# Moving the weight splits of a decoder trunk from GpSimd to VectorE, with a fifth pair of split slots

## The chip, the core and the metric

The kernel runs on one core of a Trainium2 chip. The metric is the device time of one execution in microseconds (us). The engines are TensorE (PE in the profile; PEld is its weight load), VectorE (DVE), ScalarE (ACT), GpSimd (POOL) and the queue SP, which issues the transfers from HBM.

## What is computed

A two-layer decoder trunk on 256 tokens of width 1024, all in float32. Cut to what matters here:

```python
for layer in range(2):
    main = short_conv_mixer(...) if layer == 0 else moba_attention(...)   # 12 x 64 wide
    mem_out = memory_cross_attention(q_mem, mem_k, mem_v)                 # 4 heads
    mix = concat([main, mem_out]) @ w_o[layer]
    x = layer_norm(alpha * x + mix, ln1_g[layer], ln1_b[layer])
    ffn = swiglu(x, w_gu_dense, w_down_dense) if layer == 0 else moe_swiglu(x, ...)  # top 2 of 8
    x = layer_norm(alpha * x + ffn, ln2_g[layer], ln2_b[layer])
    if layer == 0:
        shared = shared_key_value(x, w_kv_shared, cos, sin)
```

## The kernel before

**Products.** All products before the experts are made from numbers that are split in two parts: a value is `hi + lo`, each of which TensorE multiplies in one fast pass, and a product is hi·hi + lo·hi + hi·lo. Activations are split as they are made (`split`, L222). Weights are split piece by piece: a piece is 128 x 2048 numbers (1 MB). The experts, from the last norm on, take their weights whole and are not split.

**The stream of weights.** The class `Stream` (L67) holds the list of all pieces in the order of their use. A piece is loaded by SP into a raw slot (`load`), cast to `hi` by ScalarE (`high`, L129), and its `lo = raw - hi` is made by a subtraction (`low`, L139), which frees the raw slot and issues the next load. `hi` and `lo` together are a pair of split slots; there are 3 raw slots and 4 pairs (3 in `ring`, a fourth, `split4`, in `act`), and in the dense stage 2 more raw slots (`raw1`, L631). `done` frees a pair after the last product with the piece and calls `pump`, which makes as many `high` and `low` as there are free pairs, with the newest `low` left for the next call (`lag`). `held` stops `pump`; `lows` makes up all outstanding `low`; `step` makes one `high` and its `low`; `get` hands out the next piece. A pair that comes free after the last split becomes two raw slots for the experts, unless it was retired. All engines work through their instructions in the order of the program.

**Which engine subtracts.** `low` runs on VectorE, or on GpSimd while the counter `spare` is positive; `spare` is set to 2 ahead of the norms of the first layer (L643, L722) and to 8 in the attention stage (L816) and ahead of the last norm (L850). In the first step of the experts, `row_parts(0)` (L905) makes the `lo` of 128 token rows on GpSimd, `row_parts(1)` on VectorE.

**The stages around the change.** Tokens come in two blocks of 128 rows, block 0 and block 1.

- Output projection of layer 0 and its norm (L629 to L653): four pieces; the last two for block 0 first, then `layer_norm(x1[:, 0])` on VectorE while TensorE does block 1, then `layer_norm(x1[:, 1])`. TensorE goes on with `mem_keys`, in whose middle it turns block 0 (`trans_split`), and with `mem_values`, at whose end it turns block 1.
- Dense SwiGLU (L707 to L716): 11 groups of two up pieces and one down piece.
- The last three down pieces and the second norm (L717 to L732): the same pattern. After `layer_norm(x2[:, 0])` block 0 is turned, the keys' product of block 0 begins, and in its third piece block 1 is turned (task of L790).
- Keys, queries (L786 to L807), value rows with the first attention units (L815 to L819), output projection of layer 1 with the other units (L821 to L853). A unit is a pair of heads: `scores` (maximum on VectorE, exponentials on ScalarE, scaling on VectorE), `transp`, `values`. The units and `trans_split` share four PSUM banks (`bank`, L61).
- The last norm, the router and eight experts (from L848). Here raw slots are also the pools `raw2`, `raw3` and `raw5`.

Of the kernel before, what the change touches and what calls it, by code (L numbers as in the profile page):

```python
# [45 lines left out]
def trunk_kernel(ctx: ExitStack, tc: tile.TileContext, x, mem, positions, w_in_a, conv_a, w_q_b,  # L46
                 w_kv_shared, w_mem_kv, w_o, ln1_g, ln1_b, ln2_g, ln2_b, w_gu_dense, w_down_dense,
                 w_router, w_gu_moe, w_down_moe, out):
    nc = tc.nc
    pool = lambda n, **k: tc.tile_pool(name=n, bufs=1, **k)  # L50
# [16 lines left out]
    class Stream:  # L67
# [4 lines left out]
        def __init__(self):  # L72
            self.specs, self.parts, self.raw = [], {}, {}
            self.pools, self.split_pools, self.home, self.turned = [], [], {}, {}
            self.n_dma = self.n_hi = self.n_lo = self.n_got = self.n_done = 0
            self.held = False
            self.spare, self.lag = 0, 1
            self.n_split = 0

        def add(self, *specs):  # L80
# [52 lines left out]
        def low(self):  # L133
            raw, n, p = self.raw.pop(self.n_lo)
            q = self.home[self.n_lo]
            lo = q[0].tile([P, PC], F32R, name="lo", tag="lo" + q[1], bufs=q[4])
            hi = self.parts[self.n_lo][0]
            v = lo[:, :n].rearrange("p (a b) -> p a b", a=hi.shape[1])
            (nc.gpsimd if self.spare > 0 else nc.vector).tensor_sub(  # L139
                v, raw[:, :n].rearrange("p (a b) -> p a b", a=hi.shape[1]), hi)  # L140
            self.spare -= 1
            self.parts[self.n_lo].append(v)
            self.n_lo += 1
            p[3] -= 1
            self.load()
# [91 lines left out]
    def trans_split(src, hi, lo, tb, halves=(0, 1)):  # L237
        for h in halves:
            pt = bank()
            for i in range(4):  # L240
                nc.tensor.transpose(pt[:, i * P:(i + 1) * P], src[:, (4 * h + i) * P:(4 * h + i + 1) * P],
                                    identf)
            ptv = pt.rearrange("p (a b) -> p a b", a=4)
            split(hi[:, 4 * h:4 * h + 4, tb * P:(tb + 1) * P], lo[:, 4 * h:4 * h + 4, tb * P:(tb + 1) * P], ptv)

    def last(gen, tasks=(), every=1):

        tasks, v = list(tasks), None
        for i, v in enumerate(gen):
            if i % every == every - 1 and tasks:  # L250
                t = tasks.pop(0)
                if t:
                    t()
        for t in tasks:
            if t:
                t()
        return v

    def prod_ws(n, nb, ah, al):

        v = [b.rearrange("p (i t) -> p i t", i=2) for b in banks(nb // 2)]
        kt = 0
        for _ in range(n):
            w_hi, w_lo = st.get()[0]
            for k in range(w_hi.shape[1]):
                for i in range(nb):
                    w_h, w_l = w_hi[:, k, i * P:(i + 1) * P], w_lo[:, k, i * P:(i + 1) * P]
                    mm(v[i // 2][:, i % 2], w_h, ah[:, kt], start=(kt == 0 and i % 2 == 0))
                    mm(v[i // 2][:, i % 2], w_h, al[:, kt], start=False)
                    mm(v[i // 2][:, i % 2], w_l, ah[:, kt], start=False)  # L270
                kt += 1
                if k + 1 < w_hi.shape[1]:
                    yield v
            st.done()
            yield v
# [75 lines left out]
    def layer_norm(dst, old, add, gb, mid=None):  # L351
        mv = small.tile([P, 1, 2], F32, name="ln_mv", tag="ln_mv", bufs=2)
        stats = ln_sums(dst, old, add)
        if mid:
            mid()
        nc.vector.bn_aggr(mv[:, 0], stats)
        z = ln_scale(mv, 1)
        for h in range(2):
            ln_apply(dst, slice(h * 512, (h + 1) * 512), mv[:, 0, 0:1], z, gb)
# [263 lines left out]
    def wo_prod(l, dst, pc, i, tb, done, **kw):  # L623
        k0 = W_O_ORDER[l][i]
        sl = slice(tb * P, (tb + 1) * P)
        last(prod_ts(dst, pc, lambda k: mh[:, k0 + k, sl], lambda k: ml[:, k0 + k, sl], first=(i == 0), done=done,
                     **kw))

    x1 = res.tile([P, TB, D], F32, name="xt", tag="xt", bufs=2)  # L629
    more = ExitStack()  # L630
    raw1 = st.slots(more.enter_context(pool("more")), "raw1", 2)  # L631
    st.load()
    dst = [banks(), banks()]
    pcs = []
    for i in range(2):
# [4 lines left out]
    for i in (2, 3):  # L640
        wo_prod(0, dst[0], pcs[i], i, 0, False, outer=(i == 3))
    st.lows()
    st.spare = 2  # L643
    layer_norm(x1[:, 0], xt[:, 0], dst[0], gb)
    for i in (2, 3):
        wo_prod(0, dst[1], pcs[i], i, 1, True, outer=(i == 3))
    st.lows()
    with st.hold():
        layer_norm(x1[:, 1], xt[:, 1], dst[1], gb,
                   lambda: mem_keys([None] * 5 + [lambda: trans_split(x1[:, 0], xh, xl, 0)]))  # L650
        gb = ln_vectors(act, ln2_g[0], ln2_b[0])
        mem_values(tasks2=[None] * 7 + [lambda: trans_split(x1[:, 1], xh, xl, 1)])
# [18 lines left out]
    def down(g, pc, tb, done, **kw):  # L671
        hh, hl = hT[g]
        sl = slice(tb * P, (tb + 1) * P)
        last(prod_ts(dn[tb], pc, lambda k: hh[:, k, sl], lambda k: hl[:, k, sl], first=(g == 0), done=done,
                     **kw))
# [31 lines left out]
    for g in range(NG):  # L707
        up(g)
        if g == 2:
            rope_tables()  # L710
        if g == NG - 2:
            st.retire(raw1)
        if 0 < g <= NG - TAIL:
            pc = st.get()[0]
            for tb in range(TB):
                down(g - 1, pc, tb, tb == 1)  # L716
# [2 lines left out]
    for i in range(TAIL):  # L719
        down(NG - TAIL + i, pcs[i], 0, False, outer=(i == TAIL - 1))  # L720
    st.lows()
    st.spare = 2  # L722
    layer_norm(x2[:, 0], x1[:, 0], dn[0], gb)
    for i in range(TAIL):
        down(NG - TAIL + i, pcs[i], 1, i < TAIL - 1, outer=(i == TAIL - 1))
    st.lows()
    layer_norm(x2[:, 1], x1[:, 1], dn[1], gb, lambda: trans_split(x2[:, 0], xh, xl, 0))
    st.done()
    st_ffn.close()
    st.drop(raw1)  # L730
    more.close()
    gb = ln_vectors(act, ln1_g[1], ln1_b[1])  # L732

# [22 lines left out]
    def rope(pt, tb):  # L756
        t = att.tile([P, 12, HD], F32, name="roped", tag="roped", bufs=2)
        a = att.tile([P, 12, 2, 8], F32, name="rot")
        tf = t.rearrange("p h d -> p (h d)")
        nc.scalar.copy(tf[:, :512], pt[0])  # L760
        nc.scalar.copy(tf[:, 512:], pt[1][:, :MIX - 512])
        for s in range(2):
            nc.vector.tensor_tensor(a[:, :, s], t[:, :, 8 * (1 - s):8 * (1 - s) + 8],
                                    sn[:, tb, s][:, None, :].to_broadcast([P, 12, 8]), op=OP.mult)
        nc.vector.tensor_tensor(t[:, :, 0:16], t[:, :, 0:16],
                                cs[:, tb].rearrange("p a b -> p (a b)")[:, None, :].to_broadcast([P, 12, 16]),
                                op=OP.mult)
        nc.vector.tensor_tensor(t[:, :, 0:16], t[:, :, 0:16], a.rearrange("p h a b -> p h (a b)"), op=OP.add)
        return tf
# [13 lines left out]
    def turn_task(store, tb, i0, n, keys):  # L783
        return lambda: turn_heads(store[tb], tb, i0, n, keys)
# [3 lines left out]
    for tb in range(TB):  # L788
        pt = banks()
        last(token_prod(pt, pcs, tb, late=(tb == 0)), [] if tb else [None] * 9 + [lambda: trans_split(x2[:, 1], xh, xl, 1)])  # L790
        kt[tb] = rope(pt, tb)
    v = last(prod_ws(1, 2, xh, xl), [None, turn_task(kt, 0, 0, 4, True), None, turn_task(kt, 0, 4, 2, True)])
    nc.scalar.copy(qm, v[0])
    units = mem_units(att)
# [18 lines left out]
        nc.vector.tensor_copy(vb[:, tb, 512:], pt[1][:, :MIX - 512])  # L813

    u = units[2:]  # L815
    st.spare = 8  # L816
    value_rows(0, [None, None, None, None, None, turn_task(qt, 1, 0, 4, False), turn_task(qt, 1, 4, 2, False), None,
                   u[0].scores, None, None, None, u[1].scores])
    value_rows(1, [None, u[0].transp, None, None, u[2].scores, None, None, u[1].transp])  # L819
# [27 lines left out]
    st.load()  # L847
    x3 = res.tile([P, TB, D], F32, name="xt", tag="xt", bufs=2)  # L848
    wo_prod(1, dst[0], pcs[3], 3, 0, False, outer=True)
    st.spare = 8  # L850
    layer_norm(x3[:, 0], x2[:, 0], dst[0], gb)
    wo_prod(1, dst[1], pcs[2], 2, 1, True)
    wo_prod(1, dst[1], pcs[3], 3, 1, True, outer=True)  # L853
# [48 lines left out]

    def row_parts(tb):
        nc.scalar.copy(xth[:, tb], x3[:, tb])
        (nc.vector if tb else nc.gpsimd).tensor_sub(xtl[:, tb], x3[:, tb], xth[:, tb])  # L905

    def select():
        other, own = lg[:, :, None, :].to_broadcast(T4), lg[:, :, :, None].to_broadcast(T4)
# [86 lines left out]
    def experts(part):  # L995
# [159 lines left out]
        def first_step(gathers):  # L1155
            pt = banks(2)
            first_columns(pt[0], 0, 0, KT)
            logits(0)
            turn_rows(1)
            first_hidden(0, pt[0])  # L1160
            logits(1)
            select()
            row_parts(1)
            row_parts(0)
            first_columns(pt[1], 1, 0, 6)
            number()
            count()
            first_columns(pt[1], 1, 6, KT)
            for _ in range(2):
                st.passed()  # L1170
            gathers[0]()
            choose()
            for t in gathers[1:1 + KT]:
                t()
            load_orders()
            first_hidden(1, pt[1])
            load_count(0)
# [121 lines left out]
```

## Time and profile before

| | us |
|---|---|
| median of 3 runs | 1166.44 (1165.89 to 1167.29) |
| the profiled execution | 1166.54 |
| its span, first to last instruction | 1164.7 |
| TensorE, share of the span with a matmul running | 93% |
| VectorE, ScalarE, GpSimd | 33%, 22%, 6% |
| span until the first expert's products | about 477 |

How to read it: a row of the timeline gives the start in us from the span's start, the duration, the engine, the line of the kernel, the operation, the tile written and the tile read, and in brackets how long the engine sat idle ahead of it and what ended that idle time. PEclk is the granted clock of TensorE as a share of its full 2.4 GHz; its other level in this trace is 1.2 GHz (0.5).

### The profile page before, as it was taken

To read this page: it belongs to the slowest core of one execution; us is meant where nothing else is said; L and a number is where in the kernel's file an instruction comes from. 1 tells how busy PE (TensorE), PEld (TensorE's weight loads), DVE (VectorE), ACT (ScalarE), POOL (GpSimd) and SP (SyncE) were. 2 spreads that over 40 slices of the span, in tenths; PEclk is the share of its full clock that TensorE was granted. 3 is DMA by queue.
4 is the path that set the end of the run, shared out by engine and by line. 5 is a ranking of instruction groups with operands and counts; after the bars stand their busy time and mean duration, and the time that the engine had idled before them with its cause. 6 is when DMAs were issued, how large, how long until landed. Compare 5 with 4: busy or idle time off the path is not lost. (4 is left out here: it accounts for less than half of the span.)

```text
span 1164.7 us, 17138 instructions
## 1 busy us (share of the span) xinstructions
PE 1082.7 (93%) x6958; PEld 643.8 (55%) x6958; DVE 386.6 (33%) x607; ACT 256.0 (22%) x379; POOL 69.8 (6%) x55
## 2 busy tenths in 40 slices
PE   8999899999989889998988999899999999999992
PEld 7988899999877656444522443344333343343331
DVE  5767656444776566310100100101110101110105
ACT  4553443443335342110100100100100100100100
POOL 1002100000120330100000000000000000000001
PEclk9999999999989989999999999999999999999996
DMA  9646655555243239889999999989999999989992
GB/s 330 215 178 221 210 186 181 175 187 195 95 153 131 86 103 382 351 329 408 406 406 408 407 406 409 400 328 398 391 404 409 406 406 408 406 345 401 407 404 81
DMA packets 127589, 353.78 MB, mean 304 GB/s; under 512 B 6375, under 2 KB 41968, under 8 KB 127488
## 3 DMA queue, kind: packets, MB, share of 16 engines
q1 hardware_dynamic: 127392, 352.35, 79.6%
q8 instruction: 69, 1.13, 0.4%
q14 instruction: 32, 0.26, 0.1%
q0 software_dynamic: 96, 0.04, 0.0%
HBM read 351.32 MB, written 1.05 MB: 303 GB/s over the span
## 5 line engine op out<-in xcount | busy, mean ns | idle before, releaser
L65 PE MATMUL pa<-raw,xg 128*64 128x512 f32 (+4 forms) x2304 | 388.8, 560 | 9.8 <-DMA raw<-in_w_gu_moe_dram 9.3
L65 PEld LDWEIGHTS pa<-raw,xg 128*64 128x64 f32 (+1 forms) x2304 | 140.3, 129 | 245.8 <-issue 212.4
L65 PE MATMUL pb<-raw,hT 128*64 128x512 f32 x704 | 158.8, 601 | 6.9 <-ACTq L1194 2.9
L129 ACT CAST hi<-raw 128x2048 fp32r<-128x2048 f32 (+2 forms) x68 | 124.7, 1836 | 139.2 <-PE pa L65 96.8
L65 PE MATMUL pa<-xh,hi 128*128 128x256 f32 x528 | 150.0, 284 | 0.2 <-ACT xh L223 0.2
L65 PE MATMUL pa<-xl,hi 128*128 128x256 f32 x528 | 148.8, 282 | 0.3 <-DVE xl L224 0.3
L65 PE MATMUL pa<-xh,lo 128*128 128x256 f32 x528 | 148.6, 281 | 0.0
L1060 DVE TENSOR_TENSOR h<-h,pa 128x512 f32<-128x512 f32 (+2 forms) x24 | 15.3, 637 | 400.3 <-PE pa L65 388.8
L139 DVE TENSOR_TENSOR lo<-raw,hi 128x2048 fp32r<-128x2048 f32 (+2 forms) x60 | 130.5, 2181 | 48.8 <-ACT hi L129 48.8
L65 PEld LDWEIGHTS pb<-raw,hT 128*64 128x64 f32 x704 | 49.9, 138 | 102.2 <-issue 89.9
L1059 ACT ACTIVATE h<-pa 128x512 f32<-128x512 f32 (+2 forms) x24 | 13.4, 557 | 408.8 <-PE pa L65 408.8
L65 PEld LDWEIGHTS pa<-xh,hi 128*128 128x128 f32 x528 | 100.2, 190 | 1.6 <-issue 0.8
L65 PEld LDWEIGHTS pa<-xl,hi 128*128 128x128 f32 x528 | 100.2, 190 | 0.9 <-DVE xl L224 0.5
L65 PEld LDWEIGHTS pa<-xh,lo 128*128 128x128 f32 x528 | 100.1, 190 | 0.0
L139 POOL TENSOR_TENSOR lo<-raw,hi 128x2048 fp32r<-128x2048 f32 x8 | 37.7, 4726 | 370.0 <-ACT hi L129 263.1
L1207 POOL MEMSET yh<- 32x1024 f32 x8 | 7.6, 944 | 626.9 <-PE pb L65 617.5
L65 PE MATMUL pb<-raw,hTx 128*32 128x256 f32 x704 | 40.3, 380 | 3.9 <-DVE hTx L1096 3.9
L224 DVE TENSOR_TENSOR yl<-pb,yh 64x512 fp32r<-64x512 f32 (+1 forms) x32 | 17.7, 555 | 69.0 <-ACT yh L223 69.0
L65 PE MATMUL pa<-hi,xh 128*128 128x512 f32 (+1 forms) x96 | 36.1, 376 | 0.0
L1078 DVE TENSOR_TENSOR hx<-hx,pa 64x512 f32<-64x512 f32 (+1 forms) x12 | 7.8, 646 | 82.5 <-ACT hx L1077 65.3
L65 PEld LDWEIGHTS pb<-raw,hTx 128*32 128x32 f32 x704 | 22.5, 110 | 21.4 <-DVE hTx L1096 4.4
L65 PE MATMUL pa<-lo,xh 128*128 128x512 f32 (+1 forms) x96 | 33.5, 349 | 0.0
(238 smaller groups left out, 1054.7 us busy)
## 6 DMA issues: line engine op xcount, KB each, us to landing
raw<-in_w_gu_moe_dram SPq DMA_DIRECT2D x128, 1024.0 KB, 17.9
raw<-in_w_down_moe_dram SPq DMA_DIRECT2D x88, 1024.0 KB, 16.6
raw<-in_w_gu_moe_dram SPq DMA_DIRECT2D x56, 768.0 KB, 15.7
raw<-in_w_gu_dense_dram SPq DMA_DIRECT2D x44, 512.0 KB, 4.9
raw<-in_w_down_dense_dram SPq DMA_DIRECT2D x11, 1024.0 KB, 5.1
raw<-in_w_in_a_dram SPq DMA_DIRECT2D x8, 1024.0 KB, 9.9
raw<-in_w_o_dram SPq DMA_DIRECT2D x8, 1024.0 KB, 4.8
raw<-in_w_kv_shared_dram SPq DMA_DIRECT2D x6, 1024.0 KB, 5.1
```

What stands on the lines that cost most here:

```text
L65: nc.tensor.matmul(o, l, r, start=start, stop=stop, skip_group_check=True)
L129: nc.scalar.copy(hi[:, :n], raw[:, :n])
L139: (nc.gpsimd if self.spare > 0 else nc.vector).tensor_sub(v, raw[:, :n].rearrange("p (a b) -> p a b", a=hi.shape[1]), hi)
L224: nc.vector.tensor_sub(lo, src, hi)
L1059: nc.scalar.activation(h[:, :w], pg[:, :w], AF.Silu)
L1060: nc.vector.tensor_tensor(h[:, :w], h[:, :w], pu[:, :w], op=OP.mult)
L1078: nc.vector.tensor_tensor(h[64:, :w], h[64:, :w], px[64:, :w], op=OP.mult)
L1207: nc.gpsimd.memset(t[HALF:CAP].bitcast(F32), 0.0)
```

## The change

It makes all `low` run on VectorE (the counter `spare` is gone) and `row_parts(0)` too, which also moves to an earlier place. The two extra raw slots of the dense stage give way to a fifth pair of split slots of the same size (`split5`), which is the first to be filled. Between the two norms of a sub-layer of layer 0 no split is made: `held` is set ahead of the first norm, for the first sub-layer until block 1 has been turned, for the second until the keys' product of block 0 and its `rope`; there, one `step` stands between the sums and the rest of the second norm.

```diff
@@ low @@
-            (nc.gpsimd if self.spare > 0 else nc.vector).tensor_sub(
+            nc.vector.tensor_sub(
                 v, raw[:, :n].rearrange("p (a b) -> p a b", a=hi.shape[1]), hi)
-            self.spare -= 1
@@ first sub-layer @@
-    raw1 = st.slots(more.enter_context(pool("more")), "raw1", 2)
-    st.load()
+    split5 = st.split_slots(more.enter_context(pool("more")), "5", 1)
+    st.split_pools.insert(0, st.split_pools.pop())
...
     st.lows()
-    st.spare = 2
-    layer_norm(x1[:, 0], xt[:, 0], dst[0], gb)
-    for i in (2, 3):
-        wo_prod(0, dst[1], pcs[i], i, 1, True, outer=(i == 3))
-    st.lows()
     with st.hold():
+        layer_norm(x1[:, 0], xt[:, 0], dst[0], gb)
+        for i in (2, 3):
+            wo_prod(0, dst[1], pcs[i], i, 1, True, outer=(i == 3))
         layer_norm(x1[:, 1], xt[:, 1], dst[1], gb,
                    lambda: mem_keys([None] * 5 + [lambda: trans_split(x1[:, 0], xh, xl, 0)]))
@@ second sub-layer @@
-            st.retire(raw1)
+            st.retire(split5)
...
     st.lows()
-    st.spare = 2
+    st.held = True
     layer_norm(x2[:, 0], x1[:, 0], dn[0], gb)
     for i in range(TAIL):
-        down(NG - TAIL + i, pcs[i], 1, i < TAIL - 1, outer=(i == TAIL - 1))
-    st.lows()
-    layer_norm(x2[:, 1], x1[:, 1], dn[1], gb, lambda: trans_split(x2[:, 0], xh, xl, 0))
-    st.done()
+        down(NG - TAIL + i, pcs[i], 1, True, outer=(i == TAIL - 1))
+
+    def mid():
+        trans_split(x2[:, 0], xh, xl, 0)
+        st.step()
+
+    layer_norm(x2[:, 1], x1[:, 1], dn[1], gb, mid)
     st_ffn.close()
-    st.drop(raw1)
+    st.drop(split5)
+    st.split_pools.remove(split5)
@@ keys @@
         kt[tb] = rope(pt, tb)
+        if tb == 0:
+            st.held = False
+            st.pump()
@@ attention, last norm @@
-    st.spare = 8
...
-    st.spare = 8
@@ router @@
-        (nc.vector if tb else nc.gpsimd).tensor_sub(xtl[:, tb], x3[:, tb], xth[:, tb])
+        nc.vector.tensor_sub(xtl[:, tb], x3[:, tb], xth[:, tb])
...
             turn_rows(1)
+            row_parts(0)
             first_hidden(0, pt[0])
             logits(1)
             select()
             row_parts(1)
-            row_parts(0)
```

## Rows read from the trace of the kernel before

**Rows 1.** Page, part 1: busy time, share of span, instructions of each engine.

```profile
PE 1082.7 (93%) x6958; PEld 643.8 (55%) x6958; DVE 386.6 (33%) x607; ACT 256.0 (22%) x379; POOL 69.8 (6%) x55
```

**Rows 2.** Stretches: start:end, length, busy of PE, PEld, DVE, ACT, POOL, PEclk, DMA share, GB/s.

```profile
507.50:510.00 2.50, 2.50 (x15) 0.86 (x10) 0.00 (x0) 0.29 (x1) 0.00 (x0) 1.00 0.08 33
```

**Rows 3.** Waits of PE by what released them: total us, times, longest.

```profile
PE pb L241 <- DVE xt L343: 6.8, 2, 6.4
...
PE pb L774 <- DVE roped L768: 3.6, 1, 3.6
PE pb L65 <- DVE ml L224: 2.9, 1, 2.9
PE pb L401 <- ACT prob L385: 1.9, 1, 1.9
```

**Rows 4.** Timeline of POOL, its subtractions in three stages.

```profile
109.83 9.76 POOL L139 TENSOR_TENSOR lo<-raw,hi 128x2048 fp32r<-128x2048 f32 x2 [103.21 <-DMA raw<-in_w_down_dense_dram]
...
379.75 4.55 POOL L139 TENSOR_TENSOR lo<-raw,hi 128x2048 fp32r<-128x2048 f32 x1 [51.38 <-ACT hi L129]
...
409.25 9.04 POOL L139 TENSOR_TENSOR lo<-raw,hi 128x2048 fp32r<-128x2048 f32 x2 [3.71 <-DVE probT L408]
```

**Rows 5.** Timeline of DVE at the times of those subtractions.

```profile
110.12 5.12 DVE L342 SCALAR_TENSOR_TENSOR xt<-xt,ln_mv,ln_gb 128x512 f32<-128x512 f32 x1
...
380.45 4.13 DVE L763 TENSOR_TENSOR rot<-roped,sn 128x96 f32<-128x96 f32 x2 [0.96 <-ACT roped L761]
...
410.46 3.38 DVE L381 TENSOR_SCALAR sm_m<-sm_m 128x4 f32<-128x4 f32 x1
```

**Rows 6.** Stretches of 5 us, columns as in rows 2: the granted clock after the waits.

```profile
120.00:125.00 5.00, 4.80 (x29) 4.80 (x30) 4.76 (x13) 1.75 (x3) 0.00 (x0) 0.67 0.69 210
...
320.00:325.00 5.00, 0.02 (x1) 0.02 (x1) 4.96 (x3) 0.00 (x0) 4.94 (x2) 0.63 0.55 210
...
385.00:390.00 5.00, 4.49 (x18) 3.69 (x19) 0.36 (x1) 0.96 (x2) 0.00 (x0) 0.66 0.64 213
...
420.00:425.00 5.00, 5.00 (x15) 3.00 (x14) 1.56 (x4) 0.87 (x5) 0.00 (x0) 0.63 0.57 202
```

**Rows 7.** Groups by line: count, busy us, mean ns of one, idle time before.

```profile
L139 DVE TENSOR_TENSOR lo<-raw,hi 128x2048 fp32r<-128x2048 f32 (+2 forms) x60 | 130.5, 2181 | 48.8 <-ACT hi L129 48.8
```

**Rows 8.** Timeline of PE about the two norms of layer 0.

```profile
120.20 1.12 PE L241 MATMUL pb<-identf,xt 128*128 128x128 f32 x4 [4.88 <-DVE xt L343]
...
309.62 0.63 PE L65 MATMUL pb<-hi,hh 128*128 128x512 f32 x2
...
318.01 0.60 PE L241 MATMUL pb<-identf,xt 128*128 128x128 f32 x4
...
333.92 0.66 PE L241 MATMUL pb<-identf,xt 128*128 128x128 f32 x4 [0.47 <-DVE xt L343]
```

**Rows 9.** Timeline of DVE and ACT about the second norm of layer 0.

```profile
313.49 0.74 DVE L342 SCALAR_TENSOR_TENSOR xt<-xt,ln_mv,ln_gb 128x512 f32<-128x512 f32 x1
...
328.67 0.20 DVE L356 BATCH_NORM_AGGREGATE ln_mv<-ln_st 128x2 f32<-128x12 f32 x1
...
333.11 0.75 DVE L343 SCALAR_TENSOR_TENSOR xt<-xt,rs_z,ln_gb 128x512 f32<-128x512 f32 x1
...
318.64 0.59 ACT L223 CAST xh<-pb 128x512 fp32r<-128x512 f32 x1 [1.27 <-PE pb L241]
326.62 1.90 ACT L129 CAST hi<-raw 128x2048 fp32r<-128x2048 f32 x1
```

**Rows 10.** Timeline of DVE and PE in the attention stage.

```profile
399.98 0.28 DVE L408 COPY probT<-pb 128x128 f32<-128x128 f32 x1
407.41 0.18 DVE L388 RECIPROCAL sm_s<-sm_s 128x4 f32<-128x4 f32 x1 [1.85 <-ACT prob L385]
...
419.47 1.22 PE L65 MATMUL pb<-kb,qT 128*128 128x256 f32 x2 [2.89 <-DVE ml L224]
```

**Rows 11.** Transfers by line: count, KB each, median us from issue to landing.

```profile
raw<-in_w_gu_dense_dram SPq DMA_DIRECT2D x44, 512.0 KB, 4.9
```

More of the change, by code (lines that the diff above doesn't have):

```diff
@@ L76, in __init__ @@
             self.held = False
-            self.spare, self.lag = 0, 1
+            self.lag = 1
             self.n_split = 0
```

## The prediction

> **What bounds the kernel now.** I read the busy shares first, then TensorE's waits, then the stretches of the expert stage. A matmul runs during 93% of the span [rows 1], so time is won only where TensorE waits or where its clock is low; VectorE and ScalarE, at 33% and 22%, matter only where TensorE waits for them. From about 513 us on the experts' transfers and TensorE bound each other in turn, and this part only moves as a whole: at 507.5 to 510 us the transfers stand still (8% busy) because all raw slots are full [rows 2], so that until there TensorE's own progress decides. What TensorE gains before 507 us, the end gains.
>
> Ahead of that point the list of waits names VectorE nearly every time: 6.8 us for x2 in the second sub-layer, 3.6 us for the rotated queries, then 1.9 and 2.9 us in the output projection of layer 1 [rows 3]; in the first sub-layer 4.9 us for x1 stand at the matmul itself [rows 8]. Each lies behind GpSimd subtractions [rows 4]: the norm's step of 512 columns, 0.75 us elsewhere [rows 9], took 5.12 us at 110.12, in the middle of the GpSimd pair at 109.83; two rotations took 4.13 us beside the one at 379.75; a scaling of 4 numbers took 3.38 us beside the pair at 409.25, the largest of three such rows there [rows 5]. VectorE stands still until GpSimd has ended its instruction. After each wait the granted clock is at its lower level, 1.2 GHz: shares of 0.67, 0.63 (first of two such stretches), 0.66 and 0.63 over 5 us [rows 6]; a share of 0.67 is 3.3 us at half.
>
> **The change part by part.**
>
> First sub-layer. Without GpSimd beside it the norm of x1 block 0 needs 0.75 us twice more from 110.12, so it ends at 111.6. TensorE has turned its first half by 115.3 and goes on with the second at 120.2, after 4.9 us of wait [rows 8]; the wait goes, and with it the clock's fall: of the 3.3 us at half [rows 6] some 3.1 hold work, which costs 1.55 us. Gain 4.9 + 1.55 = 6.4. What is late next: the norm of block 1. From 111.6 its sums take 2.8 us, its aggregation to its end 5.2 us (328.67 to 333.86 in the other norm [rows 9]) with the two `xl` between, so it ends near 122.3; TensorE comes for it after 60 matmuls of 256 columns (0.12 us each, half of the 0.233 worked out below) and the second half's turn, 115.3 + 7.2 + 0.4 = 122.9. The splits held back cover themselves: up piece 0a is split before the norms; 0b is cast after the turn of block 1 and its `low` ends near 128.9, while TensorE works on 0a until about 129.6. That is a margin of 0.7 us. Bounds: gain 5 to 6.4 us.
>
> Dense stage. Five pairs for four and three raw slots for five. TensorE has no wait here, so a fifth pair wins nothing; the cost is nothing too as long as loads arrive. A load is issued when the `low` of the piece three places ahead of it is done; with one piece per 5.7 us it has about two pieces, 11.4 us, less that `low`'s 2.3 [rows 7], until ScalarE casts it: 9.1 us against a landing of 4.9 us [rows 11]. If that cover went, each of 33 pieces would pay.
>
> Second sub-layer. The norm of x2 block 0 without GpSimd: two halves of 1.5 us from 313.49 [rows 9], ended at 316.4, ahead of TensorE's turn at 318.01 [rows 8]. So the wait of 6.4 us for it goes. But the new `step` stands in the norm of block 1. VectorE ends the sums at 319.6 and the two `xl` at 320.9; ScalarE casts (0.59 us twice from 318.64, then 1.9 us for the piece [rows 9]) until 321.7; the `low` runs until 324.0; aggregation to end 5.2 us, so block 1 is normed at 329.1, its first half at 327.6. TensorE starts the keys at 319.2 and has 24 matmuls of 512 columns and 3 of half that before it turns block 1. One costs 0.233 us (36 of them from 309.62 to 318.01 [rows 8]), so it arrives at 325.2 and waits 2.5 us for the first half and 1.0 for the second. It goes on at 329.15 where it went on at 333.92 [rows 8]: gain 4.8. The new wait is as long as the 3.6 us one that was followed by 3.4 us at the low clock [rows 3, 6], so I take off 1.2 (between 0 and 3.4): 3.6. If neither wait nor low clock came, 8.4. Bounds 1.4 to 8.4. Queued behind the `step` on VectorE is only this norm; on SP a load that nobody awaits yet.
>
> Queries. The rotation at 380.45 takes 1.2 us in place of 4.13 and more [rows 5]; it is done at 381.7, as TensorE arrives. The wait of 3.6 us goes, and the low clock after it, 3.4 us at half, 1.7 us [rows 3, 6]. Gain 5.3. Bounds 3.6 to 5.3.
>
> Attention and output projection of layer 1. Here four `low` move onto VectorE, and they stand in the program between the units: one after u0's transposition, one after u2's scores, two after u1's transposition, all ahead of the maxima of u3. From the end of u0's copy, 400.3 [rows 10] less 5.3: 395.0; then 2.28 (`low`) + 1.3 (u2's maxima) + 2.0 (exponentials, the 1.85 us of idle [rows 10]) + 1.0 + 2.28 + 0.6 + 4.5 (two `low`) + 0.4 + 1.3 (u3's maxima), together 15.5: u3's exponentials start at 410.5. Before, they started at 413.84 (410.46 + 3.38 [rows 5]), 3.3 us later. TensorE needs the banks of these scores for u2's transposition. It comes there 5.3 us earlier, so its wait of 1.9 us [rows 3] grows to 1.9 + 5.3 - 3.3 = 3.9. Then it waits for the `ml` of u0, which VectorE makes behind u3's scaling; that is shorter by 2.2 us, the stretch of the third of those long rows. So u4's scores start 3.3 + 2.2 = 5.5 us ahead of 419.47 [rows 10], and 5.3 of these came from the queries: the stage itself gains 0.2, since the four `low` on VectorE cost it about what GpSimd's blocking cost. The clock can fall for 3.4 us or for 6.8 as before [rows 6]; I add 0.3. Take 0.5, bounds -1.5 and 6.9 (both waits gone, 4.8, and the low clock over the 4.2 us after 419.47, 2.1).
>
> Last norm and router. `spare` at L850 moves nothing, since all pieces are split by then. `row_parts(0)` goes to VectorE, 1.2 us as its twin, and is done with all selections before TensorE's next use of them: 0. Since the pair of `split4` now holds the last piece, two expert pieces are loaded one piece earlier; with the raw slots full at 507.5 us anyway [rows 2] that is 0.
>
> Sum: 6.4 + 3.6 + 5.3 + 0.5 = 15.8. The profiled execution took 1166.54, which is 0.1 above the median of the runs: 1166.54 - 15.8 = 1150.7, as a median 1150.6.
>
> **The rivals.**
>
> VectorE becomes the bound in attention. If GpSimd's subtractions there had cost VectorE nothing, the four `low` would add 4 x 2.28 = 9.1 us [rows 7] to the chain ahead of u3's maxima: 1150.6 + 9.1 = 1159.7, and half of it gives 1155. With the other terms at their low ends (5, 1.4, 3.6) and attention at -0.5 it is 1157. For it: VectorE is the chain there, and a margin of 0.7 us in the first sub-layer. Against it: the stretched rows of this very stage [rows 5]. The Trainium skill, Perfetto Trace Analysis, section Optimizing Scalar/DVE Operations, speaks for this rival: where VectorE is saturated, moving work to GpSimd may make sense, though it adds that the two share a port and that it might not help. The stretched rows bear out the second half of that rule.
>
> All waits go. If neither the `step` nor the four `low` held TensorE up: 6.4 + 8.4 + 5.3 + 6.9 = 27, 1139.5; with one of the two places, about 1145. For it: TensorE's other work could be reordered by the banks; against it: the order of the program puts the `low` ahead.
>
> The dense stage starves (slower). With three raw slots a load must land within 9.1 us. From that point each further us costs 1 us in each of 33 pieces; at 10.1 us the kernel takes 1150.6 + 33 = 1184. For it: slots cut from five to three. Against it: 4.9 us to land [rows 11].
>
> It doesn't do what it says. Were VectorE's long rows no effect of GpSimd, all would stay at 1166.4, within 0.2%. Against it: each long row ends within 0.5 us of the end of a GpSimd subtraction, a pair's first one being its half [rows 4, 5].
>
> **How the numbers follow.** Forecast 0.66 (1147 to 1155), VectorE as the bound 0.16, all or more waits go 0.08, starving 0.06, nothing 0.04. Something like 0.2% (2.3 us) is what a measurement of this kernel can tell from no change. Faster 0.90, same 0.04, slower 0.06. The range holds the forecast, nearly all of the first rival and the near half of the second: 1144.5 to 1159.
>
> **What would show it.** No subtraction on GpSimd; all L342 and L343 rows of 512 columns near 0.75 us; no wait for x1; a wait for x2 of some 3.5 us in two parts, in front of the turn of block 1; no wait for the rotated queries; in the output projection a wait of about 4 us for u3's probabilities, with four `low` ahead of u3's maxima; the transfers' pause near 500 us longer. The prediction is wrong if a wait for `lo` or `hi` appears in the dense stage, if the experts' part from 507 us on changes its length by more than 2 us, or if the rows of VectorE stay long.

## The result and the profile after

The changed kernel takes 1150.8 us (median, 1149.32 to 1152.42) against 1166.87 for the kernel before in the same comparison: a ratio of 0.9865, interval 0.985 to 0.988. The forecast was 1150.6. The line numbers of the changed kernel are one lower in this part: L240 is L241 of before, L341 and L342 are L342 and L343, L400 is L401.

The busy shares of the changed kernel answer to [rows 1], and its group of subtractions to [rows 7].

```profile
PE 1079.8 (94%) x6958; PEld 640.7 (56%) x6958; DVE 374.0 (33%) x616; ACT 255.4 (22%) x379; POOL 31.7 (3%) x46
...
L139 DVE TENSOR_TENSOR lo<-raw,hi 128x2048 fp32r<-128x2048 f32 (+2 forms) x68 | 148.5, 2194 | 48.9 <-ACT hi L129 48.8
```

The first surprise for a reader stands here: VectorE does 8 weight subtractions more than before, which is 18.0 us more of L139, and yet its busy time falls, from 386.6 to 374.0 us. Its other rows have lost 30 us. GpSimd's busy time falls from 69.8 to 31.7 us.

Where TensorE waited between 90 and 450 us, in the changed kernel (released by; total us, times, longest), the two longest waits of that stretch:

```profile
PE pb L400 <- ACT prob L384: 4.1, 1, 4.1
PE pb L240 <- DVE xt L342: 2.9, 2, 2.1
```

Against [rows 3], the wait for the rotated queries and the one for `ml` are gone, the wait for x2 has shrunk from 6.8 us to 2.9, and the wait for u3's probabilities has grown from 1.9 to 4.1 (u0 to u5 are the six units of the main attention of layer 1; `xl` and `ml` are the `lo` parts of the turned x and of the mixer's output).

To see where the time was won, I compare the start of the same matmul in both traces. TensorE's timeline before (start, duration, engine, line, operation, tiles, count, idle time before):

```profile
88.11 0.63 PE L65 MATMUL pa<-hi,mh 128*128 128x512 f32 x2
...
130.48 0.38 PE L65 MATMUL pa<-xh,hi 128*128 128x256 f32 x1 [0.24 <-ACT xh L223]
...
389.48 0.63 PE L65 MATMUL pb<-kb,qT 128*128 128x256 f32 x2
...
450.11 0.60 PE L865 MATMUL pb<-identf,xt 128*128 128x128 f32 x4
...
473.02 0.77 PE L65 MATMUL pb<-so,xth 128*128 128x192 f32 x2
```

The same matmuls after the change, with the turn of x2 block 1 (322.39 and 323.84, the second answers to 333.92 in [rows 8]) and the first product behind the long wait of the attention stage:

```profile
89.52 0.64 PE L65 MATMUL pa<-hi,mh 128*128 128x512 f32 x2
...
125.41 0.39 PE L65 MATMUL pa<-xh,hi 128*128 128x256 f32 x1 [0.24 <-ACT xh L222]
...
322.39 0.66 PE L240 MATMUL pb<-identf,xt 128*128 128x128 f32 x4 [2.07 <-DVE xt L342]
323.84 0.66 PE L240 MATMUL pb<-identf,xt 128*128 128x128 f32 x4 [0.80 <-DVE xt L342]
...
375.66 0.60 PE L65 MATMUL pb<-kb,qT 128*128 128x256 f32 x2
...
402.38 0.55 PE L400 MATMUL pb<-identf,prob 128*128 128x128 f32 x3 [4.12 <-ACT prob L384]
...
404.77 1.22 PE L65 MATMUL pb<-kb,qT 128*128 128x256 f32 x2
...
434.24 0.61 PE L867 MATMUL pb<-identf,xt 128*128 128x128 f32 x4
...
457.18 0.77 PE L65 MATMUL pb<-so,xth 128*128 128x192 f32 x2
```

Each difference of two starts is what has been won up to there:

| from the start up to | before | after | won so far | won in the stage |
|---|---|---|---|---|
| first output-projection matmul of layer 0 | 88.11 | 89.52 | -1.41 | -1.41 |
| start of the dense stage | 130.48 | 125.41 | 5.07 | 6.48 |
| turn of x2 block 1, second half | 333.92 | 323.84 | 10.08 | 5.01 |
| u0's scores (keys, queries) | 389.48 | 375.66 | 13.82 | 3.74 |
| first turn of x3 (attention, projection) | 450.11 | 434.24 | 15.87 | 2.05 |
| first gather of an expert's tokens | 473.02 | 457.18 | 15.84 | -0.03 |

The 1.41 us lost at the very start are not the change's: no edit lies there, in another trace of the changed kernel the same matmul starts at 88.20, and the last section comes back to them. From the first gather to the last matmul the experts take 671.5 us before (1144.48 - 473.02) and 671.0 after (1128.16 - 457.18): the experts' part moved as a whole.

### The profile page after: what moved, and what is told of

It is laid out like the page before. It is cut to its first block, busy times and chain, and to the rows that moved or that the text cites. A ratio compares the mean times of both kernels' runs of the same rounds, so it can differ in the third digit from the quotient of the medians.

```text
span 1150.2 us, 17136 instructions
## 1 busy us (share of the span) xinstructions
PE 1079.8 (94%) x6958; PEld 640.7 (56%) x6958; DVE 374.0 (33%) x616; ACT 255.4 (22%) x379; POOL 31.7 (3%) x46
## 5 line engine op out<-in xcount | busy, mean ns | idle before, releaser
L65 PE MATMUL pa<-raw,xg 128*64 128x512 f32 (+4 forms) x2304 | 384.6, 555 | 9.3 <-DMA raw<-in_w_gu_moe_dram 8.9
L65 PEld LDWEIGHTS pa<-raw,xg 128*64 128x64 f32 (+1 forms) x2304 | 136.1, 128 | 245.6 <-issue 216.2
L65 PE MATMUL pb<-raw,hT 128*64 128x512 f32 x704 | 161.7, 611 | 6.9 <-ACTq L1196 2.9
L139 DVE TENSOR_TENSOR lo<-raw,hi 128x2048 fp32r<-128x2048 f32 (+2 forms) x68 | 148.5, 2194 | 48.9 <-ACT hi L129 48.8
L65 PE MATMUL pa<-hi,xl 128*128 128x512 f32 (+1 forms) x96 | 32.7, 345 | 0.0
L222 ACT CAST yh<-pb 64x512 fp32r<-64x512 f32 (+1 forms) x32 | 15.1, 472 | 67.5 <-PE pb L65 54.9
```

The source lines that it names most:

```text
L65: nc.tensor.matmul(o, l, r, start=start, stop=stop, skip_group_check=True)
L139: nc.vector.tensor_sub(v, raw[:, :n].rearrange("p (a b) -> p a b", a=hi.shape[1]), hi)
L222: nc.scalar.copy(hi, src)
```

## The experiments

The theory: GpSimd's subtractions blocked VectorE, so TensorE waited and then ran at the low clock; taking them off GpSimd is the gain, and the held splits with the fifth pair are needed to collect it. The main rival: the order of the splits (the hold, the fifth pair, the `step`) is what counts, on whichever engine they run.

**The engine alone.** This is the kernel before with one edit, in `low`:

```
-            (nc.gpsimd if self.spare > 0 else nc.vector).tensor_sub(
+            nc.vector.tensor_sub(
```

> The kernel before, in which only the engine of the weight subtractions is changed: all 68 on VectorE. Two extra raw slots, four pairs, splits between the norms as before; row_parts(0) stays on GpSimd. Theory A (GpSimd's blocking of VectorE is most of the gain): the long L342 and L343 rows of the two norms go back to 0.75 us, the waits for the rotated queries and the clock loss behind it go (5.3 us), attention gains about 2 as in the changed kernel; but the two subtractions that now stand on VectorE between the norms (4.6 us) delay the norm of block 1, which gives a wait of about 2 us for x1 and one of some 3 us for the xl of x2. Sum: 4 + 2 + 5 + 2 = 13 us faster than before, about 1153.5. Theory B (the held splits and the fifth pair are what counts): within 4 us of before, above 1162.

Measured: 1149.93 us (1149.57 to 1151.19) against 1165.24, ratio 0.9865 (0.9847 to 0.9883). That is the whole gain of the change, not the smaller part that either theory allowed. TensorE's waits in this kernel, from 88 to 450 us, the two longest behind that for u3's probabilities, which is 4.1 us as in the changed kernel:

```profile
PE pa L65 <- DVE xl L224: 2.7, 1, 2.7
PE pb L241 <- DVE xt L343: 1.6, 2, 0.9
```

With the splits left between the norms, TensorE waits 1.6 us for x1 (in the first sub-layer) and 2.7 us for `xl` (in the second); the change has 0 and 2.9 in their place. So the reordering takes away a wait of 1.6 us and puts one of about the same length in the place of the other.

To see whether these 1.5 us last, both kernels ran again side by side.

> The kernel before with all weight subtractions on VectorE, once more, beside the changed kernel on one chip, to tell what the rest of the change is worth. Its trace reached the first gather of the experts at 458.8 us, that of the changed kernel at 457.2; 0.7 us of clock start speak against the latter, half of which counts. Theory A (the held splits and the fifth pair win the 2 us that the traces show): 1 to 2.5 us slower than the changed kernel. Theory B (they win nothing that lasts): within 1 us of it.

> The changed kernel beside the one above on the same chip. Theory A: 1 to 2.5 us faster than it, some 15.5 us faster than before. Theory B: the same as it within 1 us.

Measured: 1150.29 (1149.92 to 1153.0) for the engine alone and 1150.53 (1149.12 to 1151.02) for the whole change, ratios 0.9862 (0.9846 to 0.9879) and 0.9864 (0.9846 to 0.9882). So all edits but that of the engine in `low` (`row_parts(0)` stays on GpSimd in the first of the two) together win nothing that this measurement can tell.

**Attention's four subtractions back on GpSimd.** The changed kernel, in which the `low` of the value rows and behind them run on GpSimd again:

```
-            nc.vector.tensor_sub(
+            (nc.gpsimd if self.pool else nc.vector).tensor_sub(
...
     u = units[2:]
+    st.pool = True
```

> The changed kernel, in which the four subtractions from the value rows on run on GpSimd again, and nothing else. Theory A (GpSimd blocks VectorE): the wait of 3.6 us for the rotated queries comes back with its low clock, 5.3 us, and the attention stage loses the 2 us that it gained (1.1 of them low clock): about 7 us slower than the changed kernel, 1158. Theory B (the swap is even and the rotation's wait came from elsewhere): within 1.5 us of the changed kernel, 1150 to 1152.

Measured: 1155.71 (1152.85 to 1155.92) against 1165.24, ratio 0.9916 (0.9898 to 0.9934): about 6 us of the gain are gone (0.0051 of 1165). The trace is that of the fastest of the four executions, 1152.85. GpSimd and VectorE at the first of the four subtractions:

```profile
367.66 4.55 POOL L139 TENSOR_TENSOR lo<-raw,hi 128x2048 fp32r<-128x2048 f32 x1 [50.86 <-ACT hi L129]
...
368.37 4.12 DVE L764 TENSOR_TENSOR rot<-roped,sn 128x96 f32<-128x96 f32 x2 [0.98 <-ACT roped L762]
```

TensorE's waits in the same kernel:

```profile
PE pb L775 <- DVE roped L769: 3.6, 1, 3.6
PE pb L65 <- DVE ml L223: 2.9, 1, 2.9
PE pb L400 <- ACT prob L384: 1.9, 1, 1.9
```

The two rotations, 0.43 us in the changed kernel (at 371.87), take 4.12, and the last three waits of [rows 3] are back with the same lengths. This settles the first rival of the prediction: four subtractions of 2.28 us in VectorE's chain cost less than what GpSimd did to that chain. VectorE is the engine waited for in this stage, but it isn't saturated: in the changed kernel it is busy for 25.9 of the 40 us from 365 to 405. The rule of the Trainium skill that the prediction weighed (Perfetto Trace Analysis, Optimizing Scalar/DVE Operations) offers GpSimd where VectorE is saturated, so this run doesn't test it; the caution that the Trainium skill adds there, that such a move might not help since the two share a port, agrees with the 6 us.

**Without the fifth pair.** The changed kernel with the four lines of `split5` taken out, the splits still held:

```
-    split5 = st.split_slots(more.enter_context(pool("more")), "5", 1)
-    st.split_pools.insert(0, st.split_pools.pop())
...
-        if g == NG - 2:
-            st.retire(split5)
...
-    st.drop(split5)
-    st.split_pools.remove(split5)
```

> The changed kernel without the fifth pair of split slots: four pairs, three raw slots. The prediction put a fifth pair at nothing in the dense stage itself. Theory A (the pair pays for the hold: it is what lets up piece 0a be split ahead of the norms, and the keys' third piece by the step): without it the split of 0a stands behind the hold, cast 126.2 to 128.1 and subtracted until 130.4, so TensorE waits about 5 us at the start of the dense stage, with 1.6 us of low clock; the keys' third piece is split only after the norm of x2 block 1, 2 us more. About 8.5 us slower than the changed kernel, 1159; inside the dense stage no wait. Theory B (the pair wins nothing): within 1.5 us of the changed kernel.

Measured: 1158.83 (1157.68 to 1161.52) against 1165.24, ratio 0.9951 (0.9934 to 0.9967), some 10 us slower than the change (0.0086 of 1165). TensorE's waits for `lo` from 90 to 345 us, beside one of 3.0 for `hi`:

```profile
PE pa L65 <- DVE lo L139: 7.2, 3, 4.4
```

Where the longest of them and the one for `hi` lie, on TensorE's timeline:

```profile
126.53 0.58 PE L65 MATMUL pa<-xh,hi 128*128 128x256 f32 x1 [3.01 <-ACT hi L129]
...
330.20 0.39 PE L65 MATMUL pa<-lo,xh 128*128 128x256 f32 x1 [4.36 <-DVE lo L139]
```

And the 5 us about the wait for `hi` (columns as in [rows 2]):

```profile
125.00:130.00 5.00, 1.94 (x7) 1.65 (x8) 3.52 (x3) 5.00 (x3) 0.00 (x0) 0.57 0.26 90
```

TensorE works during 1.94 of these 5 us, and at a granted clock of 0.57. All waits for split pieces (the other two are 1.53 us at 128.85 and 1.32 at 322.89) stand at the ends of the two stretches in which splits are held back, and none within the dense stage. So the hold has a price, about 10 us, and the fifth pair pays it: with four pairs too few pieces are split ahead to last over the norms. Together with the run above, the fifth pair is worth 10 us only because the splits are held; held splits and fifth pair together are worth nothing.

**What GpSimd does to VectorE.** Two kernels test the mechanism by itself. Both are the changed kernel with useless GpSimd work beside the first norm, once reading two tiles in SBUF and writing one, once only writing it; none of them is used by the norm. The small subtraction that sets the start stands in both.

```
+    hi_ = st.parts[st.n_hi - 1][0]
+    nc.gpsimd.tensor_sub(zT[:, 0, :256], zT[:, 1, :256], hi_[:, 0, :256].bitcast(F32))
+    for _ in range(4):
+        nc.gpsimd.tensor_sub(zT[:, :, :256], zT[:, :, :256], cT)
```

and, in the second, in place of the loop:

```
+    for _ in range(10):
+        nc.gpsimd.memset(zT, 0.0)
```

> The changed kernel with work of no use on GpSimd beside the norm of x1 block 0: one small subtraction that sets the start (behind the cast of up piece 0a), then four subtractions of 128x1536 with two inputs from memory, about 3.6 us each, from about 103.5 to 118. They write a tile that is no longer read; the output is that of the changed kernel. Theory A (VectorE stands still while GpSimd runs an instruction that reads two tiles from memory): the four L341 and L342 rows of the norm, 0.75 us each without it, take up to 3.6 us, and a wait of 2 to 6 us for x1 comes back. Theory B (only the weight subtractions did it, by their slots or tiles): all rows stay at 0.75 us.

> The same start and the same place, with ten fills of 128x1548 zeros on GpSimd in place of the four subtractions: about 14 us of GpSimd work that writes and reads nothing. The output is that of the changed kernel. Theory A (what blocks VectorE is that both read memory): the norm's rows stay at 0.75 us and no wait for x1 appears. Theory B (any GpSimd instruction blocks VectorE): the rows take up to 1.4 us each, and the norm ends 2 to 3 us later.

Measured, in one execution each: 1158.82 with the reading instructions and 1149.74 with the writing ones, beside 1164.15 for the kernel before. GpSimd and VectorE with the reading ones:

```profile
105.61 13.06 POOL L645 TENSOR_TENSOR zT<-zT,cT 128x1536 f32<-128x1536 f32 x4
...
106.28 0.67 DVE L330 SCALAR_TENSOR_TENSOR xt<-xt,pa 128x512 f32<-128x512 f32 x1
...
108.14 0.15 DVE L303 TENSOR_SCALAR rs_i<-ln_v 128x1 int32<-128x1 int32 x1
...
109.07 3.07 DVE L308 SCALAR_TENSOR_TENSOR rs_u<-rs_z,ln_v 128x1 f32<-128x1 f32 x1
112.18 0.16 DVE L312 SCALAR_TENSOR_TENSOR rs_z<-rs_u,rs_z 128x1 f32<-128x1 f32 x1
...
115.74 3.48 DVE L341 SCALAR_TENSOR_TENSOR xt<-xt,ln_mv,ln_gb 128x512 f32<-128x512 f32 x1
```

TensorE's waits for x1 there:

```profile
PE pb L240 <- DVE xt L342: 4.9, 2, 4.6
```

The same with the writing ones:

```profile
104.83 14.44 POOL L645 MEMSET zT<- 128x1548 f32 x10
...
108.21 0.22 DVE L308 SCALAR_TENSOR_TENSOR rs_u<-rs_z,ln_v 128x1 f32<-128x1 f32 x1
...
109.18 0.74 DVE L341 SCALAR_TENSOR_TENSOR xt<-xt,ln_mv,ln_gb 128x512 f32<-128x512 f32 x1
```

Beside a GpSimd instruction of about 3.3 us that reads two tiles (13.06 / 4), VectorE's instruction on one number per partition (L308) takes 3.07 us, and again 3.07 at 112.37. It isn't slowed by its size; it stands until GpSimd's instruction is over. Of the four long steps of the norm only the first is stretched, to 3.48; the other three come behind the last subtraction and take 0.75. The wait of 4.9 us for x1 is back, as theory A said. L312, with two inputs as well, slips through in 0.16 us directly behind such an end. Rows with one input in SBUF (L303), or whose second input `pa` lies in PSUM (L330), are not stretched. Beside fills that read nothing, no row is. The Trainium skill, SBUF — State Buffer, section Who interferes with whom, states this: a VectorE instruction with two inputs in SBUF contends with a GpSimd instruction that reads SBUF, not with one that only writes it, and the port that they share is an exclusive lock. The rows agree, 3.07 us against 0.22 beside the fills. The two kernels differ in the kind of GpSimd instruction as well as in whether it reads, and the runs don't part the two. GpSimd is held up too: the small GpSimd subtraction of 128x256, begun 0.06 us after VectorE's `low` of 2.29 us (102.74 in the reading kernel), took 2.73 us, where each of the larger ones of 128x1536 took 3.2.

Two inputs don't account for everything in the kernel before. In the attention stage three long rows have a single input from SBUF: the scaling of 4 numbers, 3.38 us [rows 5] and 3.90 at 401.66 (0.17 elsewhere), and four scalings of 128x128 at 415.90, 3.19 (1.01 elsewhere). With the subtractions back on GpSimd they return, 3.39, 3.90 and 3.18. They too are long only beside a GpSimd subtraction, but no run here tells by what they were held.

**The wait for x2.** TensorE turns x2 block 1 in the middle of the keys' product. The changed kernel does this after the 9th task slot of the last piece; here it comes later, behind more of that product.

```
-        last(token_prod(pt, pcs, tb, late=(tb == 0)), [] if tb else [None] * 9 + [lambda: trans_split(x2[:, 1], xh, xl, 1)])
+        last(token_prod(pt, pcs, tb, late=(tb == 0)), [] if tb else [None] * 14 + [lambda: trans_split(x2[:, 1], xh, xl, 1)])
```

> The changed kernel, in which block 1 of x2 is turned five steps later in the keys' product of block 0 (1.8 us of matmuls go ahead of it). Theory A (TensorE's 2.9 us of wait there are the step's subtraction in the norm's way): the wait for the first half falls from 2.1 us to about 0.3, that for the second stays at 0.8 to 1.0: 1.8 us faster than the changed kernel, 1149. Theory B (the wait is hidden by something else that ends as late): no change, 1150.8.

Measured: 1147.83 (1146.25 to 1149.1) against 1166.56, ratio 0.9841 (0.9825 to 0.9858); the changed kernel itself, run beside it, gave 1151.1 (1150.81 to 1152.03).

> The changed kernel once more, beside the three others on the same chip: 1150.8 us, 16 us faster than before, with a spread of some 1.5 us from the moment at which the clock first rises (in the trace of before 10.7 us after the start, in that of the changed kernel 14.1).

The turn on TensorE's timeline, in this kernel:

```profile
321.68 0.66 PE L240 MATMUL pb<-identf,xt 128*128 128x128 f32 x4 [0.28 <-DVE xt L342]
323.13 0.66 PE L240 MATMUL pb<-identf,xt 128*128 128x128 f32 x4 [0.79 <-DVE xt L342]
```

The 5 us behind it (columns as in [rows 2]), in this kernel

```profile
325.00:330.00 5.00, 5.00 (x23) 4.04 (x22) 4.26 (x7) 3.91 (x3) 0.00 (x0) 1.00 0.48 156
```

and in the changed kernel:

```profile
325.00:330.00 5.00, 5.00 (x26) 4.68 (x26) 1.68 (x5) 2.07 (x4) 0.00 (x0) 0.69 0.65 206
```

A wait of 2.07 us is cut to 0.28, and the granted clock behind it is 1.00 in place of 0.69: 1.8 us of wait and, of 3.4 us at half, 1.7 us. The medians differ by 3.3 us (1151.1 - 1147.83), and the sum says 3.5.

**The wait for u3's probabilities.** Two of the four `low` that stand ahead of u3's maxima are held back until u4's scores are issued:

```
-    value_rows(1, [None, u[0].transp, None, None, u[2].scores, None, None, u[1].transp])
+    value_rows(1, [None, u[0].transp, None, None, u[2].scores, None, None, u[1].transp,
+                   lambda: setattr(st, "held", True)])
...
+    st.held = False
+    st.pump()
```

> The changed kernel, in which the split of the last piece of the output projection of layer 1 and the last two of the four subtractions are held back until u4's scores are out, so that they no longer stand ahead of u3's maxima on VectorE. Theory A (the wait of 4.1 us for u3's probabilities is these two subtractions, 4.5 us): the wait goes, u4's scores start about 4.3 us earlier, and the low clock of 3.4 us behind the wait may go too (1.7); a part of it may come back as a wait of 1 to 2 us for u5's scores. 3 to 6 us faster than the changed kernel, 1145 to 1148. Theory B (the units' own chain of maximum, exponential and scaling sets the pace): less than 1.5 us.

Measured: 1145.78 (1143.74 to 1146.34) against 1166.56, ratio 0.9814 (0.9797 to 0.9831), 5.3 us better than the changed kernel beside it (1151.1 - 1145.78). VectorE's maxima of u3 and the two subtractions now behind them:

```profile
394.81 1.01 DVE L378 TENSOR_REDUCE sm_m<-pb 128x2 f32<-128x256 f32 x2
...
404.65 4.49 DVE L139 TENSOR_TENSOR lo<-raw,hi 128x2048 fp32r<-128x2048 f32 x2
```

TensorE at u2's transposition, where the changed kernel waits 4.12 us, and at u4's, in the same kernel:

```profile
396.74 0.88 PE L400 MATMUL pb<-identf,prob 128*128 128x128 f32 x6
...
412.09 0.55 PE L400 MATMUL pb<-identf,prob 128*128 128x128 f32 x3 [0.81 <-ACT prob L384]
```

And its 5 us from 400 on:

```profile
400.00:405.00 5.00, 5.00 (x30) 3.56 (x28) 2.95 (x10) 3.14 (x9) 0.00 (x0) 1.00 0.00 2
```

In the changed kernel these maxima begin at 400.21, with the pair of subtractions of 4.48 us right ahead of them (VectorE's timeline of the changed kernel):

```profile
395.48 4.48 DVE L139 TENSOR_TENSOR lo<-raw,hi 128x2048 fp32r<-128x2048 f32 x2
...
400.21 1.01 DVE L378 TENSOR_REDUCE sm_m<-pb 128x2 f32<-128x256 f32 x2
```

with the same 5 us there:

```profile
400.00:405.00 5.00, 2.25 (x12) 1.31 (x13) 3.08 (x11) 2.54 (x12) 0.00 (x0) 0.82 1.03 369
```

The maxima come 5.4 us earlier; 1.0 of these this trace already has at u0's scores (374.69 against 375.66), so the stage wins 4.4. The wait of 4.1 us is gone: u2's transposition runs through. A new one of 0.8 us stands at u4's transposition, for the probabilities of u5, whose maxima the two subtractions now precede; the expectation had named it, with 1 to 2 us. And the clock no longer falls behind u2's transposition.

**Both.**

> Both of the two last edits in one kernel: the late turn of block 1 of x2, and the two late subtractions. Theory A: the gains add, since they lie in different stages ahead of the experts: 5 to 8 us faster than the changed kernel, 1143 to 1146. Theory B (the experts' transfers don't start earlier and take the gain back): less than the larger of the two gains.

Measured: 1142.73 (1140.09 to 1144.13) against 1166.56, ratio 0.9788 (0.9766 to 0.9809). This is the fastest version, 8.4 us below the changed kernel run beside it (1151.1 - 1142.73); the single gains, 3.3 and 5.3, add up to 8.6. What these edits take from the two waits that the change had left was thus worth what the traces said, each with the clock behind it.

## Why the prediction was right, step by step

- First sub-layer, 6.4 predicted, 6.48 measured. The wait for x1 is gone and TensorE turns it without idle time. The margin that the prediction named for up piece 0b, 0.7 us, came out at 0.65: its `low`, the first of three from 128.17 on, ends at 130.46 (2.29 us), and TensorE is done with 0a at about 131.1. A cover that wasn't named was used up: the load of 0a landed late, and ScalarE waited 2.75 us for it, so that the norm of block 0 began at 105.55 and ended at 113.51 (its last row is that of 112.76 below). TensorE turns it at 116.14, so 2.6 us of this cover were left. ScalarE, VectorE and TensorE about the first norm, in the changed kernel:

```profile
101.40 1.91 ACT L129 CAST hi<-raw 128x2048 fp32r<-128x2048 f32 x1 [2.75 <-DMA raw<-in_w_gu_dense_dram]
...
112.76 0.75 DVE L342 SCALAR_TENSOR_TENSOR xt<-xt,rs_z,ln_gb 128x512 f32<-128x512 f32 x1
...
116.14 1.03 PE L240 MATMUL pb<-identf,xt 128*128 128x128 f32 x8
...
128.17 6.69 DVE L139 TENSOR_TENSOR lo<-raw,hi 128x2048 fp32r<-128x2048 f32 x3 [1.49 <-ACT hi L129]
```

- Dense stage, 0 predicted: no wait for a load or for a split piece in it. But "a fifth pair wins nothing" is only half of the matter. It is true while splits flow; the run without it shows that the pair carries the two held stretches. The prediction costed the hold by its cover of 0.7 us and never asked how many pairs that cover takes.
- Second sub-layer, 4.8 predicted up to the turn of block 1, 5.01 measured; the new wait behind the `step` was put at 2.5 and 1.0 us and is 2.07 and 0.80. The low clock behind it came and falls into the next stage of the table, as 3.4 us at half.
- Queries, 5.3 less the 1.2 that were set aside for that clock, 4.1; measured 3.74, since the clock took 1.7 and not 1.2. In two further traces of the changed kernel the stage gains 3.82 and 2.52; in the second of these the clock is low for 6.8 us from the wait for x2 on, not 3.4. The rotation behind the former GpSimd row takes 0.43 us where it took 4.13 [rows 5].
- Attention and projection, 0.5 predicted, 2.05 measured (0.92 and 1.75 in the two further traces): the term that was mis-sized. Its mechanism held: four `low` stand ahead of u3's maxima, and the wait for u3's probabilities, put at 3.9 us, is 4.12. Two sizes were off. I left 0.7 us (2.9 - 2.2) of the wait for `ml`; nothing is left of it, and u4's scores are won to 14.70 us (419.47 - 404.77), 0.88 in the stage where 0.2 had been worked out. And the clock behind them had been low to 423.7, which is 4.2 us, and is now low to 406.6, which is 1.8; half the difference is 1.2, the measured 1.17, where I had added 0.3. Only the first of the two repeats: to u4's scores the further traces gain 0.90 and 0.88, but behind them 0.02 and 0.87, as the clock is low for 6.8 us there and not 3.4. So the 0.3 was a fair middle, and the miss that is sure is that of the wait for `ml`. Two slips of the working don't change this: the terms of the chain to u3's exponentials add up to 15.7 and not 15.5, and 3.38 us was not the largest of the three long rows (3.90 at 401.66).
- Last norm and router, 0 predicted, -0.03 measured.
- The experts: their length changed by 0.5 us. The transfers' pause was to grow longer; it moved with everything, and isn't longer (0.03 of the transfers busy at 492.5 to 495, against 0.08 in [rows 2], with shorter pauses about it). Here the prediction's sign in the profile was wrong, at no cost to the time.

The stages from 88 us to the first gather give 17.25 us (15.84 + 1.41) where 15.8 were predicted, and 16.17 and 15.75 in the two further traces (89.37 to 458.11 and 88.20 to 457.36, against 88.11 to 473.02 before); up to the turn of x2 all three agree within 0.05. Two parts were in no step: the start, 1.41 us in this trace, and the end. From the last matmul to the end of the span it is 20.2 us before (1164.7 - 1144.48) and 22.0 after (1150.2 - 1128.16), with the same instructions in both, and 21.8 and 21.6 in the two further traces. So it isn't the spread of the changed kernel's executions alone; whether it belongs to the change is open, as there is one trace of before. VectorE's first row of the output begins 16.0 us earlier than before (1151.96, 1135.92), so that 1.5 of the 1.8 us lie behind it, in the stores of the output and the end. So the agreement to 0.2 us is luck within some 2 us; the mechanism, and each stage to 1.6 us, is not.

The rivals: VectorE as the bound of attention is refuted by the run with GpSimd there. "All waits go" did not come by itself, but the runs with the later turn and the later subtractions show that the 27 us in it were too high: with 5.9 us of the two waits gone (1.8 and 4.1) and 0.8 come anew, the kernel is at 1142.73, not 1139.5, and some of the rest is a low clock that moved to another place (below). Starving did not come (no wait in the dense stage), nor did the rival of no effect (16 us won).

What the prediction did not ask is whether the change's other edits are needed. The engine alone gives the same time. The hold removes a wait of 1.6 us for x1 and, through the `step`, brings one of 2.9 where the old order has 2.7; in the traces the rest of the difference lies in where the low clock falls, and this is where I leave it open, since the two kernels' medians differ by 0.2 us.

## What to carry to other kernels

When a short VectorE row is long in one place, look for a row of another engine that ends where it ends, and price the move of that row by what its old place costs others, not by its own duration alone: 2.28 us of work on VectorE was cheaper than 4.55 us on GpSimd that nobody waited for. Then ask for each bulk operation what short one stands behind it on the same in-order engine and who waits for that: putting two subtractions behind the maxima, not ahead, won 5.3 us, a third of what the whole change had won. And if an edit needs another to pay for it (held splits and a fifth pair), time the plain version beside it: here it was as fast.

## What the runs showed of the hardware that was not expected

The length of the low clock after a wait isn't fixed by the wait. About the 4.1 us for u3's probabilities it was 3.4 us in the changed kernel (403.2 to 406.6), 6.8 us in another execution of the same kernel (402.0 to 408.8) and 6.8 us with the engine alone (402.5 to 409.3). With the engine alone it came behind the wait for `xl` too (320.6 to 324.0), but cost little there: TensorE reached the turn of x2 block 1 at 325.52, and VectorE had ended that norm at 325.43. In the kernel with both edits the clock stayed at its upper level through both of these places and fell later, behind the router's first products, for 6.8 us, as it did with the late subtractions alone; in the changed kernel it is low there for 3.4 us (447.6 to 451). Five microseconds of it, at a granted clock of 0.54, which is nearly all of them at the lower level:

```profile
440.00:445.00 5.00, 5.00 (x12) 2.69 (x12) 3.58 (x10) 1.54 (x3) 0.00 (x0) 0.54 1.03 408
```

So the low clock that goes with one wait can come back at the next one.

Nor does TensorE come to its full rate at a fixed time after the start. The last matmul of 0.41 us and the first of 0.28 stand about 10.5 us into the span before,

```profile
10.24 0.41 PE L65 MATMUL pa<-xh,lo 128*128 128x256 f32 x1
...
10.79 0.28 PE L65 MATMUL pa<-xh,lo 128*128 128x256 f32 x1
```

and about 14 us after the change, in the same series of products:

```profile
13.62 0.41 PE L65 MATMUL pa<-xh,hi 128*128 128x256 f32 x1
...
14.19 0.28 PE L65 MATMUL pa<-xh,hi 128*128 128x256 f32 x1
```

The profile's granted clock does not show this: it reads 1.00 from 5 to 15 us in both traces. That it is the clock is read from the durations alone: such matmuls take 0.42 us where the granted clock reads 0.50 (122.63 in the run with the reading GpSimd instructions) and 0.28 at 1.00. Some three microseconds more at half the rate account for the 1.41 us at 88 us of the table. In the two further traces of the changed kernel the rise comes at about 13 and 11 us, and the matmul at 89.37 and 88.20. So what rests on the clock can't be told to better than 1 or 2 us from one trace; the stage without it, up to the dense stage, gains 6.48 in all three.
